# A decoder layer with a mixture of experts: the last stage by tiles in the order of the routing groups

## The chip, the cores and the metric

The kernel runs on one core of a Trainium2 chip. The metric is the device time of one execution in microseconds (us). PE is TensorE, DVE VectorE, ACT ScalarE, POOL GpSimd and SP SyncE; each executes its own instructions in order and waits for others at semaphores. SP, ACT and POOL also issue DMAs.

## The reference

One decoder layer on 512 tokens of width 1024, fp32. What matters here is the part behind the three mixers, whose sum with the input is h:

```python
t = rmsnorm(h, norm2_g)                                  # 512 x 1024
g_w, g_idx = top_k(softmax(t @ wg + bg), 1)              # one of 4 groups
e_w, e_idx = top_k(softmax((t @ we + be)[group]), 2)     # two of its 8 experts
e_w = e_w / sum(e_w) * g_w
h = h + sum over the two experts of
        (silu(t @ w_gate[e]) * (t @ w_up[e]) * e_w) @ w_down[e]     # w_*: 1024 x 256, 256 x 1024
gate = sigmoid(rmsnorm(h, ple_norm_g) @ ple_gate_w + ple_gate_b)    # 1024 x 1024
h = h + gate * (p @ ple_proj_w)                          # p: 512 x 256
return rmsnorm(h, final_norm_g)
```

## The kernel before

The first 196 us compute the projections and mixers; up to about 241 us follow the output projection, which leaves h in four SBUF tiles `h1[t]` of 128 tokens, and the routing. For each tile the inverse rms is computed, the normalised rows go to DRAM as `tnd`, and the two experts of each token are found. `Rt` keeps columns per token (weights in three bfloat16 parts, the token's number) from which a product with a one-hot matrix makes values per slot.

Then come 16 **pairs** of experts, `i` = 0 to 15. Each expert has 64 slots, so a pair fills 128 rows. For a pair, `slots_of`, `fetch` and `slot_weights` make the slots' sums (`sl`, L920), the list `idx` of tokens and their weights `wsl`; POOL gathers the rows `xg` from `tnd` by an indirect DMA (L934); `gather_T` turns them on PE (L976) and multiplies by the norm's gain. `gate_up(i)` runs over 8 blocks k of 128 of the width, two column-tiled fp32 products of 64 slots x 512 columns each (L988); `between(i)` is called between the k and puts other work into PE's order there. Silu and a product with `wsl` and the up half make `hid` (L993, L994), PE turns it (L1010), `down(i)` multiplies by the down weights (L1020), and POOL stores the rows by `idy` to `yd` in DRAM (L1033), one row for each token and each of its two experts. Pair 15's rows are not stored: the last stage adds them by a one-hot product.

The expert weights are 96 loads of 1 MiB (`slab`, L689), issued by SP in the order in which `load_units` asks for them, each into a free buffer of a ring; a buffer is given back by `free` behind the products that read it, and a load also waits for the third load ahead of it (`AHEAD`).

The ple products, p @ ple_proj_w, stand in pairs 8 to 14 by the table `PLE` (L722), with 256 columns each; their weights are asked for at pair 6. Behind pair 15 the last stage runs: `add_y` adds the rows of `yd`, `scatter` adds pair 15, `turn` turns h (L1176), the gate weights, loaded at the end of pair 14, are split into a high and a low fp32r part (`gate_hi` on ACT, L1054, `gate_lo` on DVE, L1057), and for each of the four tiles 48 fp32r products (L1197) and the chain of `finish` (L1207 to L1218) follow. The order on PE is the order of the program (`manual_schedule`); on POOL and SP a scheduler sets it.

Of the kernel before, what the change touches and what calls it, by code (L numbers as in the profile page):

```python
# [17 lines left out]
P = 128  # L18
# [11 lines left out]
PLE = {8: 5, 9: 5, 10: 5, 11: 5, 12: 4, 13: 4, 14: 4}  # L30
# [56 lines left out]
def mixers(ctx, tc, A, K, dbg):  # L87
# [363 lines left out]
    h1 = K["h1"] = [hp.tile([P, D], F32, name=f"h1_{t}") for t in range(NT)]  # L451
# [160 lines left out]
def ffn(ctx, tc, A, K, mixh, mixl, out, dbg, stage):  # L612
# [49 lines left out]
    cmf = cw.tile([P, 448], F32, name="cmf", tag="cmf")[:, :384]  # L662
# [43 lines left out]
    pl_in, eo = [], []  # L706

    def ple_load():
        pl_in.extend((big(0), unit(F32, [P, 2, D])))
        nc.sync.dma_start(pl_in[0], A["pT"])  # L710
        nc.sync.dma_start(pl_in[1], A["ple_proj_w"])

    def ple_steps():

        pT, pW = pl_in
        for j in range(8):
            t, hf = j // 2, j % 2
            p = ps("pe", "sc")
            for c in range(2):
                for k in range(2):  # L720
                    n = hf * 512 + c * 256
                    PE.matmul(p[:, c * 256:c * 256 + 256], pT[:, k * S + t * P:k * S + (t + 1) * P], pW[:, k, n:n + 256],  # L722
                              start=(k == 0), stop=(k == 1))
                    if c == k == 1:
                        SC.activation(eo[t // 2][:, t % 2, hf * 512:hf * 512 + 512], p, AF.Copy)
                    yield

    ple_left = ple_steps()

    def ple(n):  # L730
        for _ in range(n):
            next(ple_left, None)
# [21 lines left out]
    def route_in(t, hf):  # L754
# [11 lines left out]
        SC.activation(junk, h1[t][:, hs], AF.Square, accum_out=ms2[:, hf:hf + 1])  # L766

# [5 lines left out]
    def route(t):  # L773
# [664 lines left out]
```

## Time and profile before

| | us |
|---|---|
| median of 3 runs | 557.72 |
| their range | 556.37 to 564.31 |
| the profiled execution's own time | 562.7 |
| its span (first to last instruction) | 560.9 |
| PE busy in the span | 513.1 (91%) |
| DVE, ACT, POOL busy | 276.0, 209.8, 85.3 |
| begin of pair 0, end of gate-up 15 | 241.5, 475.7 |

The numbers of a profile come from one execution, here one 5 us above the median; differences are taken within it and then set against the median. A large busy share of an engine doesn't say that the engine ends last at each place: that is read from the chain of waits, stage by stage.

### The profile page before, as it was taken

The numbers are of one execution on the slowest core, as the hardware profiler recorded it, in microseconds if no ns is written. First come the engines' busy times: TensorE is split into PE (matmuls) and PEld (weight loads), VectorE is DVE, ScalarE is ACT, GpSimd is POOL, SyncE is SP. The second block draws the span as 40 slices with busy tenths as digits, with TensorE's granted clock in tenths as the row PEclk, the third lists the DMA queues.
The fourth block names the chain that finished last, engine by engine and source line by source line (L and its number), as shares of the span: only waits on it lengthen the run. The fifth ranks groups of instructions, "written<-read, shape, count | busy, mean of one in ns | idle before, by whom it ended". The sixth has DMA issues, their size and how long they took to land.

```text
span 560.9 us, 7565 instructions
## 1 busy us (share of the span) xinstructions
PE 513.1 (91%) x2713; PEld 322.1 (57%) x2713; DVE 276.0 (49%) x727; ACT 209.8 (37%) x435; POOL 85.3 (15%) x122
## 2 busy tenths in 40 slices
PE   8899999999999999979999999099999999679992
PEld 5797886877997788934333333044434333347782
DVE  6663957757846666772422222022122112687774
ACT  7466765656857444211111111001111112363442
POOL 3301121311009400002111111001111100010000
PEclk9999999999999999998999999699999999899997
DMA  8882222300449579978999999999999999861111
GB/s 305 262 330 59 74 65 78 100 1 2 134 156 420 221 294 424 356 278 327 403 417 414 393 390 377 375 409 389 395 408 420 391 415 377 348 252 37 39 38 41
DMA packets 35641, 148.82 MB, mean 265 GB/s; under 512 B 6557, under 2 KB 13597, under 8 KB 22160
## 3 DMA queue, kind: packets, MB, share of 16 engines
q1 hardware_dynamic: 29984, 137.20, 63.6%
q0 software_dynamic: 4320, 7.95, 3.8%
q10 hardware_dynamic: 1296, 3.15, 1.4%
q8 instruction: 23, 0.38, 0.3%
q14 instruction: 18, 0.15, 0.1%
HBM read 139.61 MB, written 16.25 MB: 278 GB/s over the span
## 4 chain that ended last, share of the span: by engine, by line
PE 74%; DMA 10%; DVE 7%; ACT 5%; issue 2%; POOL 1%; SPq 0%; DVEq 0%; ACTq 0%; POOLq 0%
PE gu L988 17%; PE pj L232 9%; PE dn L1020 8%; PE po L78 8%; DMA unit<-in_w_exp_dram 5%; PE pj L255 5%; PE pg L1197 4%; PE z L255 4%; PE pe L722 3%; PE z L309 2%; DMA unit<-in_ple_proj_w_dram 2%; PE po L331 2%; DVE h L1117 2%; PE x L965 1%; DMA xg<-tnd,idx 1%
## 5 line engine op out<-in xcount | busy, mean ns | idle before, releaser
L988 PE MATMUL gu<-unit,xT 128*64 128x512 f32 x512 | 116.7, 597 | 0.0
L988 PEld LDWEIGHTS gu<-unit,xT 128*64 128x64 f32 x512 | 34.5, 136 | 62.3 <-issue 60.9
L1020 PE MATMUL dn<-unit,hidT 128*64 128x512 f32 x256 | 60.1, 612 | 1.0 <-ACT hidT L1011 0.5
L232 PE MATMUL pj<-xh,wp 128*128 128x512 f32 x176 | 51.2, 398 | 0.3 <-ACT wp L67 0.3
L1197 PE MATMUL pg<-unit 128*128 128x512 f32 (+1 forms) x216 | 49.4, 384 | 1.5 <-DVE unit L1057 1.5
L993 ACT ACTIVATE sg<-gu 128x256 f32<-128x256 f32 x16 | 6.1, 384 | 106.8 <-PE gu L988 106.8
L921 DVE COPY SL<-sl 128x10 f32<-128x10 f32 (+1 forms) x17 | 2.9, 168 | 85.0 <-PE sl L920 85.0
L1197 PEld LDWEIGHTS pg<-unit 128*128 128x128 f32 x216 | 37.9, 194 | 11.2 <-DVE unit L1057 3.4
L994 DVE SCALAR_TENSOR_TENSOR hid<-sg,wsl,gu 128x256 f32<-128x256 f32 x16 | 7.7, 480 | 74.4 <-ACT sg L993 74.4
L1033 POOL DMA_INDIRECT yd<-big,idy x15 | 15.1, 1009 | 150.4 <-ACT big L1024 150.4
L232 PEld LDWEIGHTS pj<-xh,wp 128*128 128x128 f32 x176 | 32.5, 188 | 8.1 <-ACT wp L67 1.2
L1020 PEld LDWEIGHTS dn<-unit,hidT 128*64 128x64 f32 x256 | 17.3, 140 | 33.6 <-issue 28.1
L1024 ACT ACTIVATE big<-dn 128x512 f32<-128x512 f32 x30 | 17.9, 597 | 49.6 <-PE dn L1020 49.6
L68 DVE TENSOR_TENSOR wp<-wraw,wp 128x768 fp32r<-128x768 f32 (+2 forms) x28 | 25.8, 928 | 13.6 <-ACT wp L67 13.4
L722 PE MATMUL pe<-unit,big 128*128 128x256 f32 x64 | 18.4, 420 | 13.4 <-DMA unit<-in_ple_proj_w_dram 13.4
L67 ACT ACTIVATE wp<-wraw 128x768 fp32r<-128x768 f32 (+2 forms) x28 | 22.8, 817 | 20.2 <-PE pj L232 9.8
L232 PE MATMUL pj<-xl,wp 128*128 128x512 f32 x88 | 29.4, 400 | 0.0
L78 PE MATMUL po<-wo,mx 128*128 128x512 f32 x96 | 25.6, 407 | 0.0
L255 PE MATMUL pj<-wp,xh 128*128 128x384 f32 x96 | 24.8, 351 | 0.0
L78 PE MATMUL po<-unit,mx 128*128 128x512 f32 x96 | 24.1, 400 | 0.0
L977 DVE TENSOR_TENSOR xT<-xt,g2c 128x512 f32<-128x512 f32 x30 | 20.6, 688 | 6.7 <-PE xt L976 6.7
L934 POOL DMA_INDIRECT xg<-tnd,idx x15 | 15.4, 1029 | 55.7 <-issue 35.7
(293 smaller groups left out, 878.8 us busy)
## 6 DMA issues: line engine op xcount, KB each, us to landing
unit<-in_w_exp_dram SPq DMA_DIRECT2D x96, 1024.0 KB, 9.2
wraw<-in_w_in_dram SPq DMA_DIRECT2D x20, 384.0 KB, 6.1
yd<-zero SPq DMA_DIRECT2D x4, 1024.0 KB
unit<-in_ple_gate_w_dram SPq DMA_DIRECT2D x4, 1024.0 KB
unit<-yd SPq DMA_DIRECT2D x4, 1024.0 KB, 4.8
wraw<-in_w_out_dram SPq DMA_DIRECT2D x8, 256.0 KB, 2.9
h<-in_x_dram SPq DMA_DIRECT2D x4, 512.0 KB, 4.1
unit<-in_w_out_dram SPq DMA_DIRECT2D x4, 512.0 KB, 7.9
```

Of the source, the lines that this page charges most:

```text
L67: nc.scalar.activation(h, src, AF.Copy)
L68: nc.vector.tensor_tensor(l, src, h.bitcast(F32), ALU.subtract)
L78: nc.tensor.matmul(p, a[k][:, ts_], K["wo"][k][:, b, hs], start=(n == 0), stop=(n == 3 * len(ks) - 1))
L232: PE.matmul(q, a[:, i * P:(i + 1) * P], b[k], start=(n == 0), stop=(n == 3 * KC - 1))
L255: PE.matmul(p[t][:, :W_IN[j]], a[k][:, t * P:(t + 1) * P], b, start=(n == 0), stop=(n == 3 * KC - 1))
L722: PE.matmul(p[:, c * 256:c * 256 + 256], pT[:, k * S + t * P:k * S + (t + 1) * P], pW[:, k, n:n + 256], start=(k == 0), stop=(k == 1))
L934: G.indirect_dma_start(out=xg[i % 2], out_offset=None, in_=tnd, in_offset=bass.IndirectOffsetOnAxis(ap=idx[:, i:i + 1], axis=0), bounds_ch ...
L977: V.tensor_tensor(xTs[i, hf], p.rearrange("p (a b) -> p a b", a=4), g2c[:, 4 * hf:4 * hf + 4, None].to_broadcast([P, 4, P]), ALU.mult)
L988: PE.matmul(gu[64 * e:64 * e + 64], xTs[i, k // 4][:, k % 4, 64 * e:64 * e + 64], w[e][k // 4][:, 512 * (k % 4):512 * (k % 4) + 512], star ...
L1020: PE.matmul(dn[64 * e:64 * e + 64], hT[:, f, 64 * e:64 * e + 64], w[e][2][:, 1024 * f + 512 * hf:1024 * f + 512 * hf + 512], start=(f == 0 ...
L1024: SC.activation(o[:, 512 * hf:512 * hf + 512], dn, AF.Copy)
L1197: PE.matmul(p, hT[t][:, a, ks], gw[k][:, b, hs], start=start and n == 0, stop=stop and n == len(ab) - 1)
```

## The change

Five things change together.

- **Inverse rms at the slots.** `hd` takes the place of `tnd`: the rows of h as they are, stored by ACT without waiting for the inverse rms. The inverse rms goes into three more columns of `Rt` and comes out per slot as `rsl`; `wsl` is multiplied by its square. `gate_up` ends with two ACT and two DVE instructions instead of one each.
- **Tokens ranked by group.** `ranks()` in pair 1 gives each token a rank in the order of the four groups, and stores the list through DRAM (`perm_d`) into `perm`: four indirect stores and one load, all on POOL. Rows of p, of h (`load_h`) and of yd (`load_y`) are gathered by `perm` on POOL. Tiles of the last stage are tiles of this order, so tile 0 needs no pair behind 7 and tile 1 none behind 11.
- **Where the work stands.** The table `WORK` has three numbers for a pair: steps ahead of gate-up, between its k, and behind it. A step is a group of four transposes or one product of 512 columns. ple stands in pairs 4 to 8, tile 0 of the last stage in 9 to 12, tile 1 in 13 to 15; tiles 2 and 3 follow pair 15.
- **Gate weights unsplit.** 16 fp32 products of 512 columns for a tile instead of 48 fp32r ones; the gate weights are loaded behind pair 5, in the stream of the expert loads.
- The output is stored by rows with an indirect DMA on POOL. The two buffers that held `h1` join the ring of the weights, and the longer-lived tiles (p, ple weights, gate weights, rows, h, y) take buffers of it.

```diff
-PLE = {8: 5, 9: 5, 10: 5, 11: 5, 12: 4, 13: 4, 14: 4}
+WORK = {4: (0, 3, 1), 5: (0, 3, 1), 6: (0, 3, 1), 7: (0, 3, 1), 8: (0, 1, 1),
+        9: (1, 3, 1), 10: (1, 3, 1), 11: (1, 3, 1), 12: (0, 2, 1), 13: (1, 4, 1), 14: (1, 4, 1), 15: (1, 4, 1)}
...
-        SC.activation(sg, gu[:, :256], AF.Silu)
-        V.scalar_tensor_tensor(hid, sg, wsl[:, i:i + 1], gu[:, 256:], ALU.mult, ALU.mult)
+        SC.activation(hid, gu[:, :256], AF.Copy, scale=wsl[:, i:i + 1])
+        SC.activation(sg, gu[:, :256], AF.Sigmoid, scale=rsl[:, i:i + 1])
+        V.tensor_tensor(hid, hid, gu[:, 256:], ALU.mult)
+        V.tensor_tensor(hid, hid, sg, ALU.mult)
...
+    ring.extend(((K["hp"], "h0"), (K["hp"], "h1")))
     load_units()
...
+    def ranks():
...
+        for t in range(NT):
+            G.indirect_dma_start(out=perm_d, out_offset=bass.IndirectOffsetOnAxis(ap=rki[:, t:t + 1], axis=0), in_=tok[:, t:t + 1],
+                                 in_offset=None, bounds_check=S - 1, oob_is_err=False)
+        G.dma_start(perm, perm_d.rearrange("(t p) o -> p (t o)", p=P))
...
+    def ple_load():
+        pl["p"], pl["w"] = unit(F32, [P, 2, D]), unit(F32, [P, 2, D])
+        nc.sync.dma_start(pl["w"], A["ple_proj_w"])
+        for t in range(NT):
+            rows_of(pl["p"][:, 0, t * 256:t * 256 + 256], A["p"], perm[:, t:t + 1], S)
...
+    def load_y(t):
+        if t not in ys:
+            ys[t] = unit(F32, [P, 2, D])
+        for r, ix in enumerate((perm, perm2)):
+            rows_of(ys[t][:, r], yd, ix[:, t:t + 1], 2 * S)
...
+            for k in range(KC):
+                PE.matmul(p, q["x"][:, 0, k * P:k * P + P], gr[k // 2][:, k % 2, hs], start=(k == 0), stop=(k == KC - 1))
...
+            if i == 1 and k == 6:
+                ranks()
+            if k in (1, 3, 5, 6)[:n]:
+                run(work, 1)
+            if i in (8, 12) and k == 6:
+                load_y(i // 4 - 2)
...
-        ple(PLE.get(i, 1) - 1)
+        ahead, _, behind = WORK.get(i, (0, 0, 0))
+        run(work, ahead)
         gate_up(i, between(i))
         free(*(slab[6 * i + n] for n in (0, 3, 1, 4)))
         if i == 15:
             break
-        if i == 6:
+        if i == 2:
             ple_load()
+        if i == 5:
+            for j in range(4):
+                gate_load(j)
         if i == 7:
-            eo += [unit(F32, [P, 2, D]) for _ in range(2)]
+            rows_load()
+            load_h(0)
...
         load_units()
         gather_T(i + 1, 1)
-        if i in PLE:
-            ple(1)
+        run(work, behind)
         down(i, lambda n: gather_T(i + 1, 0))
```

PE's order in pair 4, before, from the slots' sums to the down products (`gu` gate-up, `xt` a turn of xg, `ht` the turn of hid, `dn` down):

```order
L920 MATMUL sl<-pr,Dm 128x10
L988 MATMUL gu<-unit,xT 64x512 x14
L976 MATMUL xt<-ident,xg 128x128 x4
L1010 MATMUL ht<-ident,hid 128x128 x2
L976 MATMUL xt<-ident,xg 128x128 x4
L1020 MATMUL dn<-unit,hidT 64x512 x8
```

The same place in the changed kernel (L1120 turns p, L1110 is a ple product):

```order
L911 MATMUL sl<-pr,Dm 128x13
L982 MATMUL gu<-unit,xT 64x512 x2
L1120 MATMUL xt<-ident,unit 128x128 x4
L982 MATMUL gu<-unit,xT 64x512 x4
L1120 MATMUL xt<-ident,unit 128x128 x4
L982 MATMUL gu<-unit,xT 64x512 x4
L1110 MATMUL pe<-unit 128x512
L982 MATMUL gu<-unit,xT 64x512 x4
L970 MATMUL xt<-ident,xg 128x128 x4
L1110 MATMUL pe<-unit 128x512
L999 MATMUL ht<-ident,hid 128x128 x2
```

Three steps have moved between the products of gate-up, two of them turns that read the gathered p, and one between the turn of xg and that of hid.

POOL's order from pair 3 to pair 5, before (the numbered names in brackets are the DMA rings and engines that an instruction waits for):

```order
L934 DMA xg<-tnd,idx 128x1024 [waits DMASW1_49,DVE_49,PE_49]
L1033 DMA yd<-big,idy 1024x1024 [waits DMASW4_49,Activation_49]
L934 DMA xg<-tnd,idx 128x1024 [waits DMASW3_49,DVE_49,PE_49]
L1033 DMA yd<-big,idy 1024x1024 [waits DMASW6_49,Activation_49]
L934 DMA xg<-tnd,idx 128x1024 [waits DMASW5_49,DVE_49,PE_49]
```

The same stretch in the changed kernel:

```order
L925 DMA xg<-hd,idx 128x1024 [waits DMASW3_49,DVE_49,PE_49]
L1084 DMA perm<-tok,rki 512x1 [waits DMASW0_49]
L1022 DMA yd<-big,idy 1024x1024 [waits DMASW1_49,Activation_49]
L925 DMA xg<-hd,idx 128x1024 [waits DMASW6_49,DVE_49,PE_49]
L1086 DMA perm_2559<-perm 128x4x1 [waits DMASW3_49]
L1090 DMA unit<-in_p_dram,perm_2559 128x256 [waits DMASW6_49]
L1090 DMA unit<-in_p_dram,perm_2559 128x256 x2
L1090 DMA unit<-in_p_dram,perm_2559 128x256 [waits DMASW2_49]
L1022 DMA yd<-big,idy 1024x1024 [waits DMASW4_49,Activation_49]
```

The load of perm and the four gathers of p now stand behind the gather xg(6), which is issued in pair 4, and ahead of the store yd(4).

PE's order at the change from pair 8 to pair 9 in the changed kernel (L1173 turns h of tile 0, L1198 is a gate product); before, nothing stands there but gate-up, sums, turns, down and ple:

```order
L1009 MATMUL dn<-unit,hidT 64x512 x8
L1173 MATMUL xt<-ident,unit 128x128 x4
L982 MATMUL gu<-unit,xT 64x512 x2
L911 LDWEIGHTS Dm
L911 MATMUL sl<-pr,Dm 128x13
```

The first turn of tile 0 stands between the down products of pair 8 and gate-up of pair 9.

## Rows read from the trace of the kernel before

**Rows 1.** Windows: stretch, length, busy us (x instructions) of PE PEld DVE ACT POOL, PEclk, DMA, GB/s

```profile
350.00:365.00 15.00, 1.64 (x7) 0.98 (x4) 0.00 (x0) 0.60 (x1) 1.01 (x1) 0.61 0.99 378
365.00:476.00 111.00, 110.02 (x529) 44.10 (x527) 22.57 (x88) 18.89 (x38) 13.13 (x13) 0.99 1.00 403
476.00:561.00 85.00, 62.50 (x283) 46.15 (x283) 58.21 (x93) 34.73 (x68) 5.28 (x8) 0.92 0.32 125
```

**Rows 2.** Chain of waits in order of time: start us, us, what (x records)

```profile
144.60 0.86 PE z L354 x2
...
299.08 0.86 PE gu L988 x4
299.94 0.19 PE sl L920 x4
300.13 6.21 PE gu L988 x28
308.29 3.65 PE dn L1020 x16
...
352.46 11.28 DMA unit<-in_ple_proj_w_dram
363.88 3.54 PE pe L722 x8
...
380.42 1.93 PE pe L722 x8
...
395.36 1.92 PE pe L722 x8
...
473.85 1.89 PE gu L988 x8
```

**Rows 3.** Waits of the SP queue: us in total, times, longest

```profile
SPq L689 <- DMA unit<-in_w_exp_dram: 219.4, 84, 9.3
```

**Rows 4.** Waits of PE from 241 to 476 us

```profile
PE pe L722 <- DMA unit<-in_ple_proj_w_dram: 13.4, 1, 13.4
...
PE xt L976 <- DMA xg<-tnd,idx: 1.9, 1, 1.9
```

**Rows 5.** Timeline at the end of gate-up of pair 5

```profile
319.08 0.66 PE L976 MATMUL xt<-ident,xg 128*128 128x128 f32 x4
319.28 0.38 ACT L993 ACTIVATE sg<-gu 128x256 f32<-128x256 f32 x1 [6.67 <-PE gu L988]
...
319.70 0.48 DVE L994 SCALAR_TENSOR_TENSOR hid<-sg,wsl,gu 128x256 f32<-128x256 f32 x1 [5.00 <-ACT sg L993]
...
320.24 0.44 PE L1010 MATMUL ht<-ident,hid 128*128 128x128 f32 x2 [0.50 <-DVE hid L994]
```

**Rows 6.** Timeline of POOL in pair 4

```profile
300.03 1.00 POOL L1033 DMA_INDIRECT yd<-big,idy  x1 [10.12 <-ACT big L1024]
301.75 1.01 POOL L934 DMA_INDIRECT xg<-tnd,idx  x1 [0.72 <-issue]
```

**Rows 7.** Issue to landing: gathers (L934), stores (L1033), and a page row

```profile
DMA to landing us min/median/max: 4.9/8.8/11.2
...
DMA to landing us min/median/max: 7.7/8.6/9.3
...
out_dram<-unit ACTq DMA_DIRECT2D x4, 256.0 KB, 2.9
```

**Rows 8.** Timeline of the last products' chain in the last stage

```profile
549.43 0.43 DVE L1209 TENSOR_TENSOR unit<-unit 128x256 f32<-128x256 f32 x1 [0.48 <-ACT unit L1208]
...
551.65 0.48 DVE L1207 SCALAR_TENSOR_TENSOR unit<-pg,rsp,rows 128x256 f32<-128x256 f32 x1
...
554.88 0.72 ACT L1215 ACTIVATE unit<-unit,rsl 128x512 f32<-128x512 f32 x1 [0.85 <-POOL rsl L61]
...
555.64 0.34 ACTq L1216 DMA_DIRECT2D out_dram<-unit  x1
```

**Rows 9.** Groups of the last stage: out<-in xcount, busy, mean ns, idle before

```profile
L1117 DVE TENSOR_TENSOR h<-h,unit 128x1024 f32<-128x1024 f32 x8 | 9.8, 1223 | 5.3 <-DMA unit<-yd 5.1
```

More of the change, by code (lines that the diff above doesn't have):

```diff
@@ L703, in ffn @@
     load_units(2)
[L706 to L732, printed above, removed]
     V.tensor_copy(cm.rearrange("p a b -> p (a b)"), cmf)
     V.tensor_tensor(rw, rw, g2c[:, :, None].to_broadcast([P, KC, 36]), ALU.mult)
-    tnd = dram.tile([S, D], F32, name="tnd")
-    Ab = mw.tile([P, NT, 32], BF, name="Ab")
-    pr_ = cw.tile([P, 448], F32, name="pr", tag="cmf")
+    hd = dram.tile([S, D], F32, name="hd")
+    Ab = mw.tile([P, NT, 40], BF, name="Ab")
+    pre = mw.tile([P, NT, 4], F32, name="pre")
+    pr_ = cw.tile([P, 576], F32, name="pr", tag="cmf")
     posA = pr_[:, :128].rearrange("p (t e) -> p t e", t=NT)
@@ new lines, in ple_steps @@
+    def ple_steps(pT, n):
+        for j in range(8):
+            t, hf = j // 2, j % 2
+            p = ps("pe", "sc")
+            for c in range(0, 512, n):
+                for k in range(2):
+                    m = hf * 512 + c
+                    PE.matmul(p[:, c:c + n], pT(t, k), pl["w"][:, k, m:m + n], start=(k == 0), stop=(k == 1))
+                    if c + n == 512 and k:
+                        SC.activation(eo[t // 2][:, t % 2, hf * 512:hf * 512 + 512], p, AF.Copy)
+                    yield
@@ new lines, in begin, with add_y, mean_sq @@
+    def begin(t):
+        T[t] = dict(h=hs_[t], x=unit(F32, [P, 2, D], slot_of[id(ys[t])][0]), e=eo[t // 2][:, t % 2], n=t)
+    def add_y(t, rs=(0, 1)):
+        for r in rs:
+            V.tensor_tensor(hs_[t], hs_[t], ys[t][:, r], ALU.add)
+    def mean_sq(ms, m):
+        if ms is None:
+            ms = small("msq", 1)
+            V.tensor_scalar(ms, m, 1.0 / D, EPS, ALU.mult, ALU.add)
+        else:
+            V.scalar_tensor_tensor(ms, m, 1.0 / D, ms, ALU.mult, ALU.add)
+        return ms
@@ new lines, in by_group, with tile_work, all_work @@
+    def by_group(q, ot):
+        G.indirect_dma_start(out=out, out_offset=bass.IndirectOffsetOnAxis(ap=perm[:, q["n"]:q["n"] + 1], axis=0), in_=ot, in_offset=None,
+                             bounds_check=S - 1, oob_is_err=False)
+    def tile_work(t):
+        add_y(t)
+        begin(t)
+        for hf in range(2):
+            turn(T[t], hf)
+            yield
+        rms(T[t])
+        yield from finish(T[t], by_group, ((0, 512), (512, 512)), "sc")
+    def all_work():
+        yield from ple_work()
+        free(pl["p"], pl["w"])
+        for t in range(2):
+            yield from tile_work(t)
@@ L1096, in between, with count_beyond @@
+    def count_beyond():
+        on = ov["on"] = mw.tile([1, 1], I32, name="on")
+        po = ps("pov", "xt")
+        PE.matmul(po[:1, :1], ov["om"], ones[:, :1], start=True, stop=True)
+        V.tensor_copy(on, po[:1, :1])
     def between(i):
+        n = WORK.get(i, (0, 0, 0))[1]
         def go(k):
@@ L1263, in ffn, with behind_down @@
-    ov_slots = ring[:4]
-    junk, h3s = (unit(F32, shape, slot) for shape, slot in zip(([P, 2, 512], [P, 4, 512]), ring[4:]))
-    SC.preload_act_table_set("sigmoid_and_others")
-    rms(0)
-    tail(sums)
+    run(work, WORK[15][2])
+    def behind_down(n):
+        if n < 2:
+            add_y(2, (n,))
+            run(work, 1)
+    down(15, behind_down)
+    for t in (2, 3):
+        if t == 3:
+            add_y(3)
+        begin(t)
+        for hf in range(2):
+            scatter(t, hf)
+        if t == 2:
+            prep(T[2])
+            count_beyond()
```

386 lines of the change are left out of this document (214 added, 172 removed).

## The prediction, made before the changed kernel had run

> **What bounds the kernel now.** I read the windows first [rows 1]. In the second half of the expert pairs, from 365 to 476 us, PE is busy for 110.02 of 111.00 us, while the DMA share is 1.00. So PE and the weight stream are both full there, and the next view has to say which ends last. Ahead of it lies a stretch of 15 us in which PE does 1.64 us of work; in the last stage (476 to 561) PE has 62.50 of 85.00 us, DVE 58.21, and the DMA share is 0.32.
>
> The chain of waits [rows 2] gives the pair as a unit: pair 4 begins at 299.08 and ends with its down products, 3.65 us from 308.29 on, at 311.94. That is 12.86 us a pair, all PE: gate-up, the turn of hid, down. In pair 8 the chain leaves PE for the load of the ple weights, which lands at 363.74; PE waits 13.4 us [rows 4] and then needs 3.54 us for eight ple products that take 1.93 us in pair 9, with a mean granted clock of 0.61 in that stretch, part of it at the lower of the two levels (1.2 and 2.4 GHz) behind an idle PE [rows 1, 2]. From there a pair lasts 14.94 us (380.42 to 395.36). The wait list of the SP queue [rows 3] shows that the weight loads wait 219.4 us for earlier loads and little for anything else; the DMA is a second bound, just under the first. The end of gate-up in pair 15 is at 475.7 [rows 2]; the 85.2 us from there to 560.9 are the tail.
>
> **The change, part by part.** I sum in two pieces, up to the end of gate-up 15 and the tail.
>
> *Pairs, PE alone.* Without ple and its wait, pair 15 would begin at 299.08 + 11 x 12.86 = 440.5 and its gate-up, 0.86 + 0.19 + 6.21 us and a last small step [rows 2], would end at 447.9. The program before has 28 us above that: 17.0 in pair 8, the rest ple at 2 us a pair.
> An unsplit fp32 product of 512 columns on the full array is in this program already: two records at 144.60, 0.86 us [rows 2]. Put between column-tiled products it also costs a change of the array's use and back; four ten-column products with both changes cost 0.19 us at 299.94 [rows 2]. So 1.05 us for each inserted step; for a group of four transposes, 0.66 us [rows 5], I take 0.6. The step behind gate-up costs nothing: it stands where PE waits for hid (0.50 us idle there [rows 5]) and that wait grows, by the next point. hid had one ACT and one DVE instruction after gate-up (0.38 and 0.48 us), and now has two ACT and two DVE ones; the added DVE product of 128x256 at 0.43 [rows 8] and its hand-over make 0.48 us a pair, on the path.
> By WORK that gives: pair 0 -0.9 (below), 1 to 3 1.4, 4 2.7, 5 to 7 3 x 3.63 = 10.9, 8 1.5, 9 3.8, 10 and 11 2 x 4.68 = 9.4, 12 2.6, 13 4.8, 14 5.7, 15 5.25; together 47.2. Gate-up 15 ends at 495.1 if nothing waits. The -0.9: in pair 0 the first gather waits for the normalised rows; these are now stored unscaled, some 3 us earlier, and PE's wait for xg was 1.9 us in all [rows 4].
>
> *Added wait 1, rows of p.* The transposes of p stand in PE's order at the second k of pair 4, ahead of the rest of its gate-up. In pair 4 PE comes to them at 299.6 + 1.9 = 301.5. On POOL the load of perm stands behind xg(6), which before is issued at 301.75 [rows 6] and now at about 302.3, since its index comes from the same pair. perm is issued at 303.3 in the same queue. xg lands 4.9, 8.8 or 11.2 us after its issue (minimum, median, maximum) [rows 7]; at the median perm is there at about 312, then POOL issues the gathers of p one by one at 1.0 us each [rows 6], and the second, which the first group needs, goes out at 313.0. With 5.5 us, nearer to the minimum because these rows are a quarter of xg's, it lands at 318.5: a stall of **17.0 us** on PE. With 4.9 us for both steps it is 12.6, with 8.8 for p too 20.3, and below nothing it can't go, as perm can't be issued before xg(6). A stall of that kind also cost 3.54 - 1.93 = 1.6 us of clock. Behind POOL's wait are queued yd(4) and xg(7), which PE needs only two pairs later, so they cost nothing.
> The Trainium skill, "DMA: Bandwidth & Descriptors", section "Anatomy of one DMA — SWDGE (gpsimd) path", gives about 2.0 us plus the bytes at 436 GB/s for such a DMA; by that estimate xg(6) and perm land near 305.5, p at 308.7, and the stall is 7 us. The trace disagrees for this kernel: the same kind of gather took at least 4.9 us here [rows 7].
>
> *Added waits 2 and 3, rows of yd.* Tile 0 needs yd of pair 7, tile 1 that of pair 11. yd(i) is issued about 1 us after the start of the next pair (300.03 in pair 4 [rows 6]) and lands 8.6 us later [rows 7]: 9.7 us into pair 8. Only then POOL issues the two gathers; the second goes at 10.7 and lands at about 19.2, and DVE adds it in 1.22 us [rows 9]. PE wants the turned tile behind down(8), at 12.86 + 1.5 = 14.4. That is a stall of **6 us** (2.4 with landings of 4.9, 8.7 with 11.2). In pair 13 the same sum against 12.86 + 2.6 = 15.5 gives **5 us** (1.3 to 7.6). Queued behind these on POOL are yd(8) and xg(11), with a pair's slack.
>
> *Weights.* Gate weights, rows, h and y rows add 9.5 MiB ahead of the last expert load. At 403 GB/s [rows 1] that is 24.7 us on a last arrival at about 475, less 5 for the two more slots of the ring: 494.5, or 505 where the ring is full during the stall. PE with its waits comes to 495.1 + 17.0 + 1.6 + 6 + 5 = **524.7**, so the stream doesn't decide.
>
> *Tail.* hid, turn and down start 2.4 us after gate-up 15 (1.9 before, by the steps of [rows 5], plus 0.48), down takes 3.65 [rows 2], the scatter and its additions end at 9.0, the turns of tile 2 at 10.6. Then 32 products of 0.86 us and 1.3 us of transposes: 39.4. From the last product to the scaling 3.2 us (551.65 to 554.88 [rows 8]), scaling 0.6, the store by rows from POOL 6.4 us (between 4.9 and 8.8, nearer the low end since little else moves), and about 2 us from the last landing to the end as before (555.64 + 0.34 + 2.9 to 560.9 [rows 7, 8]). Together **51.5** instead of 85.2. Gone are the split of the gate weights on ACT and DVE, the wait of 5.1 us for yd [rows 9], and two of four tiles with 48 products each.
>
> Sum: 524.7 + 51.5 = 576.2 against a span of 560.9, +15.3. The profiled execution (562.7) is 5 us above the median of 557.7; I add the difference to the median: **573 us**, 2.7% slower.
>
> **The rivals.**
> A. *Short landings.* DMA work gets thinner while PE stalls, and each landing comes at the minimum of the rows, 4.9 us. Then the stalls are 12.6, 2.4 and 1.3, gate-up 15 ends at 495.1 + 12.6 + 1.6 + 3.7 = 513.0, the tail at 50.0, span 563, median about 560: no change that a measurement of this kernel can tell (about 2%). For it: the rows of p are small. Against it: the median of 15 gathers in the pairs is 8.8, beside a weight stream like this one. The skill's figure quoted above would go further, to about 551.
> B. *The other side: PE never waits.* If perm is there in pair 3, for instance because the queue issues it while xg(6) still waits for its index, p is in place at 302; and if yd lands by the middle of a pair, the turns are on time. Then only the weight stream (494.5 to 505) and PE (495.1) count, and the span is 495.1 to 505 + 51.5 = 546.6 to 556.5, median 543 to 553, about 546. It decides from a p landing below 302 on. Against it stands POOL's order, in which one engine issues all of these.
> C. *Longer.* DVE and ACT have the chains of the moved tiles to do between the hid of two pairs, on engines that execute in order; 1 us more in each of pairs 9 to 15 (a DVE instruction of 128x1024 is 1.22 us [rows 9]) and stalls at their upper ends (20.3, 8.7, 7.6) give +7 + 8.6: 588.
> That the change doesn't do what it says has no room here: the two tiles do stand in the pairs in PE's order.
>
> **How the numbers follow.** The forecast has 0.50, A 0.22, B 0.13, C 0.15. The forecast's own range is 566 to 580. The range leaves out most of B and the upper half of C: 553 to 584. More than 2% slower begins at 568.9: C and most of the forecast, 0.56; faster than 546.6 is half of B, 0.06; the rest, 0.38, is within 2%.
>
> **What would show it.** In the profile after, a wait of PE for rows of p of 10 to 20 us near 302, with a low clock behind it; waits of PE for the turned tile of about 6 us at the start of pair 9 and 5 at that of pair 13; inserted products at 0.86 us; end of gate-up 15 near 525, and 51 us behind it. I am wrong if p comes early (B), if the landings are short (A), or if weights are what PE waits for in pairs 9 to 15.

## The result and the profile after

The changed kernel took 631.15 us (627.34 to 631.93, four runs) against 558.75 for the kernel before; the ratio, by the means of all runs (six of the changed kernel), is 1.1262, 95% interval 1.118 to 1.1343. Run again later, beside the experiments, it took 626.62 us, ratio 1.1132 (1.1076 to 1.1189). It is 11 to 13% slower, where 2.7% was forecast and 584 us was the upper end of the range. The span of its profiled execution is 625.6 us; gate-up 15 ends at 556.5 instead of 475.7, and the tail behind it takes 69.1 us instead of 85.2.

Windows of the changed kernel, columns as in [rows 1]: pair 4, pair 5, pairs 8 and 9, pairs 12 and 13, and three stretches of the tail:

```profile
307.18:345.39 38.21, 18.09 (x76) 6.07 (x74) 4.29 (x18) 4.52 (x9) 6.89 (x7) 0.73 0.76 263
345.39:362.99 17.60, 16.80 (x72) 5.39 (x70) 4.11 (x17) 3.61 (x7) 2.07 (x2) 1.00 0.94 366
398.19:422.51 24.32, 15.58 (x72) 5.55 (x69) 6.66 (x20) 4.74 (x10) 5.53 (x5) 0.91 0.95 381
422.51:442.01 19.50, 18.70 (x76) 5.93 (x75) 5.47 (x20) 2.62 (x7) 1.68 (x3) 0.93 0.95 384
479.00:503.49 24.49, 16.77 (x74) 5.74 (x70) 9.73 (x26) 5.98 (x13) 7.05 (x7) 0.93 0.97 385
503.49:524.67 21.18, 20.38 (x77) 6.14 (x76) 3.92 (x9) 2.63 (x7) 3.67 (x5) 0.92 0.71 274
556.50:564.20 7.70, 1.42 (x4) 0.38 (x4) 4.56 (x9) 3.08 (x7) 0.56 (x1) 0.84 0.03 9
564.20:570.10 5.90, 5.87 (x17) 1.68 (x18) 2.29 (x3) 0.62 (x2) 1.24 (x1) 0.63 0.22 89
570.10:605.50 35.40, 30.36 (x74) 14.51 (x75) 15.49 (x28) 6.53 (x16) 2.91 (x4) 0.86 0.00 0
```

A pair that took 12.86 us now takes 17.60 with three steps between its products; pair 4 takes 38.2, with PE busy in half of it. In these three stretches of the tail PE has a granted clock of 0.63 to 0.86. The wait list of PE says where it stood, to be read beside [rows 4]:

```profile
PE xt L1120 <- DMA unit<-in_p_dram,perm: 19.3, 2, 18.7
PE ht L999 <- DVE hid L990: 16.1, 15, 2.9
PE xt L1173 <- DVE unit L1158: 14.3, 2, 7.9
PE dn L1009 <- ACT hidT L1000: 5.4, 1, 5.4
PE xt L1173 <- DVE unit L1174: 3.9, 2, 3.1
PE xt L970 <- DMA xg<-hd,idx: 3.5, 1, 3.5
```

The first is the wait for the rows of p in pair 4, the third the two for the rows of yd ahead of pairs 9 and 13 (7.9 and 6.4). The last is the wait for the first gather in pair 0, which was 1.9 us before [rows 4]. No line of it names the expert weights. POOL's timeline up to the gathers of p, where [rows 6] had a store and a gather for each pair:

```profile
294.30 0.99 POOL L1084 DMA_INDIRECT perm<-tok,rki  x1 [11.55 <-DMA perm<-tok,rki]
...
303.12 1.01 POOL L1084 DMA_INDIRECT perm<-tok,rki  x1 [5.20 <-DMA perm<-tok,rki]
...
310.05 1.04 POOL L925 DMA_INDIRECT xg<-hd,idx  x1 [0.70 <-issue]
312.26 0.82 POOL L1086 DMA_DIRECT2D perm<-perm  x1 [1.17 <-DMA perm<-tok,rki]
325.18 1.04 POOL L1090 DMA_INDIRECT unit<-in_p_dram,perm  x1 [12.10 <-DMA perm<-perm]
```

Each store of ranks waits for the landing of the one before; the load of perm waits for the last of them and then lands 12.7 us after its issue, though it is 2 KB; only then the gathers of p go out. Two rows of the DMA issues give the landings of p and perm, and the view of line L925 those of the gathers xg:

```profile
unit<-in_p_dram,perm POOLq DMA_INDIRECT x4, 2.8
perm<-perm POOLq DMA_DIRECT2D x1, 2.0 KB, 12.7
...
DMA to landing us min/median/max: 4.4/9.2/14.1
```

The longest of these gathers, 14.1 us, is xg(6), issued at 310.05, 2.2 us ahead of the load of perm in the same queue. It lands at 324.15, and perm 0.8 us behind it; in the five other traces that show both landings perm is 0.6 to 0.8 us behind xg(6) too, issued 1.5 to 3.1 us after it. The load had waited only 1.17 us for the last store of ranks. So of the chain it is mainly the place of the load behind xg(6) that makes the wait, as the traces read, and not the four stores; no run has the one without the other.

The end of gate-up in pair 5, to be set beside [rows 5]:

```profile
354.93 1.46 PE L982 MATMUL gu<-unit,xT 128*64 128x512 f32 x6
...
356.46 0.47 ACT L987 ACTIVATE hid<-gu,wsl 128x256 f32<-128x256 f32 x1 [4.23 <-PE gu L982]
356.84 0.47 ACT L988 ACTIVATE sg<-gu,rslot 128x256 f32<-128x256 f32 x1
357.02 0.69 DVE L971 TENSOR_TENSOR xT<-xt,g2c 128x512 f32<-128x512 f32 x1 [8.32 <-PE xt L970]
357.62 0.41 DVE L989 TENSOR_TENSOR hid<-hid,gu 128x256 f32<-128x256 f32 x1
358.07 0.42 DVE L990 TENSOR_TENSOR hid<-hid,sg 128x256 f32<-128x256 f32 x1
358.55 0.44 PE L999 MATMUL ht<-ident,hid 128*128 128x128 f32 x2 [0.71 <-DVE hid L990]
...
359.51 1.51 PE L1009 MATMUL dn<-unit,hidT 128*64 128x512 f32 x6
```

The kernel before at the same place, beside [rows 5] (where hid is at 319.70):

```profile
318.55 0.60 PE L988 MATMUL gu<-unit,xT 128*64 128x512 f32 x2
...
320.10 0.68 DVE L977 TENSOR_TENSOR xT<-xt,g2c 128x512 f32<-128x512 f32 x1
...
321.15 3.65 PE L1020 MATMUL dn<-unit,hidT 128*64 128x512 f32 x16
```

DVE multiplies the turned xg (L971) ahead of hid; before, hid came first. From the last product of gate-up to down it is 3.12 us (356.39 to 359.51), before 2.00 (319.15 to 321.15). It is 3.12 in pairs 2 and 3 too, where no step stands behind gate-up, so that step costs nothing here, as predicted. The start of the tail, with the chain of tile 1's second half on DVE, ACT and POOL:

```profile
558.20 0.74 DVE L1202 SCALAR_TENSOR_TENSOR unit<-pg,rsp,unit 128x512 f32<-128x512 f32 x1
558.43 0.41 PE L999 MATMUL ht<-ident,hid 128*128 128x128 f32 x2 [0.92 <-DVE hid L990]
558.98 0.63 ACT L1203 ACTIVATE unit<-unit 128x512 f32<-128x512 f32 x1 [1.61 <-DVE unit L1202]
...
561.09 0.63 ACT L1206 ACTIVATE unit<-unit 128x512 f32<-128x512 f32 x1 [1.48 <-DVE unit L1205]
...
563.29 0.61 ACT L1212 ACTIVATE unit<-unit,rsl 128x384 f32<-128x384 f32 x1 [1.48 <-POOL rsl L64]
...
563.82 0.36 ACT L1000 ACTIVATE hidT<-ht 128x256 f32<-128x256 f32 x1
564.23 5.77 PE L1009 MATMUL dn<-unit,hidT 128*64 128x512 f32 x16 [5.39 <-ACT hidT L1000]
```

The copy of the turned hid (L1000) stands behind ACT's part of that chain (L1203, L1206, L1212); PE waits 5.4 us, and the 16 records of down then take 5.77 us instead of the 3.65 of [rows 2].

### The profile page after: what moved, and what is told of

Read it like the earlier page. It is cut to its first block, busy times and chain, and to the rows that moved or that the text cites. A ratio compares the mean times of both kernels' runs of the same rounds, so it can differ in the third digit from the quotient of the medians.

```text
span 625.6 us, 7465 instructions
## 1 busy us (share of the span) xinstructions
PE 543.0 (87%) x2609; PEld 302.3 (48%) x2609; DVE 276.2 (44%) x797; ACT 199.9 (32%) x435; POOL 111.9 (18%) x147
## 3 DMA queue, kind: packets, MB, share of 16 engines
q0 software_dynamic: 6976, 16.87, 7.5%
## 5 line engine op out<-in xcount | busy, mean ns | idle before, releaser
L982 PE MATMUL gu<-unit,xT 128*64 128x512 f32 x512 | 128.6, 621 | 0.0
L1009 PE MATMUL dn<-unit,hidT 128*64 128x512 f32 x256 | 64.2, 647 | 6.5 <-ACT hidT L1000 5.4
L971 DVE TENSOR_TENSOR xT<-xt,g2c 128x512 f32<-128x512 f32 x30 | 20.7, 691 | 109.3 <-PE xt L970 109.3
L1198 PE MATMUL pg<-unit 128*128 128x512 f32 (+1 forms) x144 | 66.8, 591 | 0.0
L982 PEld LDWEIGHTS gu<-unit,xT 128*64 128x64 f32 x512 | 32.2, 139 | 69.8 <-issue 68.3
L987 ACT ACTIVATE hid<-gu,wsl 128x256 f32<-128x256 f32 x16 | 7.6, 474 | 120.2 <-PE gu L982 107.1
L1198 PEld LDWEIGHTS pg<-unit 128*128 128x128 f32 x144 | 26.2, 200 | 35.3 <-issue 34.3
L71 DVE TENSOR_TENSOR wp<-wraw,wp 128x768 fp32r<-128x768 f32 (+2 forms) x28 | 25.8, 928 | 13.8 <-ACT wp L70 13.5
L912 DVE COPY SL<-sl 128x13 f32<-128x13 f32 (+2 forms) x17 | 2.9, 171 | 51.8 <-PE sl L911 51.8
L970 PE MATMUL xt<-ident,xg 128*128 128x128 f32 x120 | 20.2, 294 | 3.5 <-DMA xg<-hd,idx 3.5
L1173 PE MATMUL xt<-ident,unit 128*128 128x128 f32 x32 | 6.5, 338 | 18.3 <-DVE unit L1158 14.3
L970 PEld LDWEIGHTS xt<-ident,xg 128*128 128x128 f32 x120 | 14.4, 149 | 14.9 <-issue 14.9
```

The source lines that it names most:

```text
L71: nc.vector.tensor_tensor(l, src, h.bitcast(F32), ALU.subtract)
L970: PE.transpose(p[:, k * P:(k + 1) * P], xg[i % 2][:, (4 * hf + k) * P:(4 * hf + k + 1) * P], ident)
L971: V.tensor_tensor(xTs[i, hf], p.rearrange("p (a b) -> p a b", a=4), g2c[:, 4 * hf:4 * hf + 4, None].to_broadcast([P, 4, P]), ALU.mult)
L982: PE.matmul(gu[64 * e:64 * e + 64], xTs[i, k // 4][:, k % 4, 64 * e:64 * e + 64], w[e][k // 4][:, 512 * (k % 4):512 * (k % 4) + 512], star ...
L1009: PE.matmul(dn[64 * e:64 * e + 64], hT[:, f, 64 * e:64 * e + 64], w[e][2][:, 1024 * f + 512 * hf:1024 * f + 512 * hf + 512], start=(f == 0 ...
L1198: PE.matmul(p, q["x"][:, 0, k * P:k * P + P], gr[k // 2][:, k % 2, hs], start=(k == 0), stop=(k == KC - 1))
```

## The experiments

Ratios are to the kernel before, run on the same chip (561 to 561.5 us). Against the second measurement of the changed kernel, 1.1132, differences under 0.6% are not told apart by the time; there the trace decides. Traces differ by chance too: pair 0 begins between 240.8 and 245.4 us, though hardly an edit touches what stands ahead of it, and gate-up 15 of the same kernel ended at 556.5 and at 558.4. The second measurement is of the unedited kernel:

> The changed kernel again, unedited, so that the other edits are set against a run beside them. Theory: its ratio to before is the first one, 1.118 to 1.134. Rival 'the first measurement lay high': the spans of the profiles (625.6 here, 623.4 and 623.5 with edits that took 2 us off the trace) say that it is nearer 1.115.

Measured 1.1132 (1.1076 to 1.1189), span 627.4: the rival is right, the first measurement lay high by about 1%. In this run the waits were 17.5, 9.9 and 7.6.

**ple one pair later.**

```diff
-WORK = {4: (0, 3, 1), 5: (0, 3, 1), 6: (0, 3, 1), 7: (0, 3, 1), 8: (0, 1, 1),
+WORK = {5: (0, 4, 1), 6: (0, 4, 1), 7: (0, 4, 1), 8: (0, 2, 1),
```

> The changed kernel with the ple work in pairs 5 to 8 instead of 4 to 8 (same steps, one pair later; only the table is edited). Theory 'PE in line' (each wait in PE's order and the low clock behind it come off the end one for one): the wait for the rows of p, 18.7 us in pair 4, falls to at most 4 us, pair 4 loses some 5 us of slow products as well, end of gate-up 15 at 532 to 536 instead of 556.5, time some 20 to 24 us shorter, near 609. Rival 'weights': the stream of weights has used that wait to get ahead; PE waits for expert weights in pairs 8 to 13 instead and the time falls by less than 10 us.

Measured 1.0992 (1.0931 to 1.1052), span 619.7, gate-up 15 at 551.6. The time fell by some 7 us (626.62 to 619.73): the rival's number, less than 10, but not for its reason, since PE's wait list names no expert weights. The wait only fell to 12.2 us, since the scheduler had also moved POOL. Its timeline in this kernel:

```profile
312.25 0.82 POOL L1086 DMA_DIRECT2D perm<-perm  x1 [1.44 <-DMA perm<-tok,rki]
321.99 1.03 POOL L1022 DMA_INDIRECT yd<-big,idy  x1 [8.92 <-ACT big L1013]
323.74 1.04 POOL L925 DMA_INDIRECT xg<-hd,idx  x1 [0.72 <-issue]
325.08 1.01 POOL L1090 DMA_INDIRECT unit<-in_p_dram,perm  x1 [0.30 <-issue]
```

The gathers of p went out at the same time as before the edit, now behind a store and a gather of the next pair, and landed 9.8 to 10.1 us later instead of 2.8. Two things differ there, and no run tells them apart: the gather xg of 512 KB stands 1.3 us ahead in the same queue (it took 10.1 us, and the first p landed 1.3 us behind it), and the DMA share is 1.00 instead of 0.28.

**Silu in pairs 0 to 7.**

```diff
-        SC.activation(hid, gu[:, :256], AF.Copy, scale=wsl[:, i:i + 1])
-        SC.activation(sg, gu[:, :256], AF.Sigmoid, scale=rsl[:, i:i + 1])
-        V.tensor_tensor(hid, hid, gu[:, 256:], ALU.mult)
-        V.tensor_tensor(hid, hid, sg, ALU.mult)
+        if i < 8:
+            SC.activation(sg, gu[:, :256], AF.Silu, scale=rsl[:, i:i + 1])
+            V.scalar_tensor_tensor(hid, sg, wsl[:, i:i + 1], gu[:, 256:], ALU.mult, ALU.mult)
+        else:
...
```

In these pairs `wsl` is the weight times the inverse rms, not its square; the other pairs keep the four lines.

> The changed kernel with the old form of hid in pairs 0 to 7: one Silu on ACT with the inverse rms as its scale, one DVE instruction with the weight times the inverse rms. Theory 'two more instructions are the 1.1 us between gate-up and down (3.1 instead of 2.0)': 3.1 goes back to 2.0 to 2.1 in eight pairs, 8 to 9 us shorter, near 622, less where the step behind gate-up (pairs 4 to 7) no longer fits under the wait: at worst 4 us shorter. Rival 'the order on DVE' (the turned xg is multiplied before hid): it stays at 2.7 or more, and the gain is under 3 us.

Measured 1.1087 (1.1029 to 1.1145), span 620.9. From gate-up to down it is 2.67 us in pairs 2 to 7, not 2.0: the two instructions are 0.45 of the 1.12 us. That is the rival's stretch; gate-up 15 ends 3.7 us earlier, between the rival's 3 and the 4 of the theory at worst. In pair 8, the first with the new form, ACT loads a table between Copy and Sigmoid (ACT_TABLE_LOAD, 1.28 us), and the stretch is 4.26.

**DVE's order at hid.**

```diff
+        with ExitStack() as behind:
+            if i > 0:
+                behind.enter_context(tc.issue_after(K["hid", i - 1].ins))
             V.tensor_tensor(xTs[i, hf], p.rearrange("p (a b) -> p a b", a=4),
...
```

> The changed kernel with DVE's order as it was before at the end of gate-up: the turned xg is multiplied behind the last product of hid, not ahead of the first. Theory 'order on DVE is 0.6 of the 1.1 us that a pair has lost between gate-up and down': 3.1 falls to about 2.5 in 15 pairs, 8 to 10 us shorter. Rival 'the two added instructions are all of it': it stays at 3.0 or more and the time doesn't move by more than 2 us.

Measured 1.1087 (1.1036 to 1.1139), span 623.4. The stretch falls to 2.84 us, 0.28 less: between the two theories, since the first product on DVE now waits for the sigmoid. With both edits (g4b_all below) it is 2.09 us in pairs 2 and 3, so the order is worth 0.6 there once the two instructions are gone; in pairs 4 to 7 it is 2.41, since the step behind gate-up no longer fits into the wait. The wait at pair 9 grew from 7.9 to 9.1 meanwhile.

**Last step of tile 1.**

```diff
-... 15: (1, 4, 1)}
+... 15: (1, 4, 0)}
```

> The changed kernel with the last step of tile 1 (its 16th product and the chain of DVE and ACT behind it) emitted behind the copy of the turned hid of pair 15 instead of ahead of it. Theory 'ACT's order': the 5.4 us for which down(15) waits go, and with them the low clock of down(15) (5.8 instead of 3.65): 6 to 8 us shorter, near 624. Rival 'the chain only moves': ACT's chain now delays the copies of down's results, and the tail gets at most 3 us shorter.

Measured 1.1177 (1.1115 to 1.124), span 623.5: no difference in the time. Gate-up 15 ends at 556.55, down starts 3.2 us later instead of 7.8 and takes 3.65, but the tail is only 2.2 us shorter: the rival. PE's wait list has this line instead:

```profile
PE sc L1255 <- ACT big L1017: 2.7, 1, 2.7
```

**Tile 0 in pairs 10 to 12.**

```diff
-        9: (1, 3, 1), 10: (1, 3, 1), 11: (1, 3, 1), 12: (0, 2, 1), 13: ...
+        10: (1, 4, 1), 11: (1, 4, 1), 12: (1, 4, 1), 13: ...
```

> The changed kernel with tile 0 of the last stage in pairs 10 to 12 (six steps each) instead of 9 to 12. Theory 'PE in line': the wait of 7.9 us ahead of pair 9 for the rows of yd goes, and with it some 1.5 us of low clock: 8 to 10 us shorter, near 622. Rival 'the wait moves': tile 0 now ends where tile 1 begins, the wait ahead of pair 13 grows or DVE delays hid in pairs 10 to 12, and at most 4 us are left.

Measured 1.0907 (1.0835 to 1.0978), span 609.6, 16 us less: more than the 8 to 10 expected. Only one wait for yd is left, ahead of pair 13, and it is smaller (2.9 us). Gate-up 15 ends 12.7 us earlier: 7.9 and 3.5 of the two waits, the rest low clock behind the first. The tail is 3.3 us shorter, for which the runs show no cause.

**p without the list.**

```diff
-            rows_of(pl["p"][:, 0, t * 256:t * 256 + 256], A["p"], perm[:, t:t + 1], S)
+            nc.sync.dma_start(pl["p"][:, 0, t * 256:t * 256 + 256], A["p"][t * P:(t + 1) * P, :])
```

> The changed kernel with the rows of p loaded by SP in the order of the tokens, as plain loads, instead of gathered by the list of ranks; the ple term is then added to the wrong tokens, so this part of the computation is changed. Theory 'the chain on POOL (four scatters, one load, four gathers, each waiting for the one before) is the wait of pair 4': the 18.7 us go, with 4 to 5 us of low clock; 20 to 24 us shorter. Rival 'the wait is only moved': the stream of weights, which was 0.76 busy during the wait, or the rows of yd at pairs 9 and 13 take most of it, gain under 10 us.

Measured 1.0857 (1.0803 to 1.0912), span 611.8. Pair 4 takes 16.66 us instead of 38.2: the wait of 18.7 and 2.9 us of low clock. But the waits for yd grow to 13.6 and 6.8, and pair 4 began 2.0 us later in this run, so that gate-up 15 ends 13.3 us earlier, not 21:

```profile
PE xt L1173 <- DVE unit L1158: 20.4, 2, 13.6
```

**The list made on PE.** The one-hot of each token's rank, built by DVE, is multiplied with the tokens' numbers (16 products, pair 2), in place of four stores and a load:

```diff
-            G.indirect_dma_start(out=perm_d, out_offset=bass.IndirectOffsetOnAxis(ap=rki[:, t:t + 1], axis=0), in_=tok[:, t:t + 1], ...)
-        G.dma_start(perm, perm_d.rearrange("(t p) o -> p (t o)", p=P))
+            V.tensor_tensor(ohx[0][:, t], iota64[:, None, :].to_broadcast([P, 8, 64]), ra[:, :, None].to_broadcast([P, 8, 64]), ALU.is_equal)
...
+                PE.matmul(pq[:, 2 * j:2 * j + 2], ohx[0][:, t, 2 * j:2 * j + 2].rearrange("p b s -> p (b s)"), Rt[:, t, 0, 6:8], ...)
```

> The changed kernel with the list of ranks turned round on PE (16 products of a one-hot matrix with the tokens' numbers in pair 2) instead of by four indirect stores and a load on POOL; p is gathered as before. Theory 'the chain of DMAs on POOL is the wait of pair 4': p is there before pair 4, the 18.7 us go with 3 us of low clock, end of gate-up 15 about 16 to 20 us earlier (some of it given back at pair 9, where without the chain the wait grew from 7.9 to 13.6 us with plain loads of p). Rival 'gathers of p are late by themselves': a wait of 8 us or more stays in pair 4.

Measured 1.0766 (1.0709 to 1.0823). In this kernel the entries lay beyond the tables (an offset of 1024 was missing), so no row was gathered or stored by the list (the POOL queue moved 7.96 MB instead of 16.87); its time leaves that traffic out. With the offset:

> The changed kernel with the list of ranks made on PE, now with the right entries. Theory 'the chain of DMAs on POOL is the wait of pair 4': no wait for p above 2 us in pair 4, gate-up 15 ends 14 to 20 us earlier (536 to 543), the wait at pair 9 is larger than the 7.9 us of the changed kernel. Rival 'gathers of p are late by themselves': a wait of 8 us or more stays in pair 4.

Measured 1.0871 (1.0817 to 1.0925), span 605.7, gate-up 15 at 538.3, 18.2 us earlier; p is there in pair 4, and the wait at pair 9 is 11.1:

```profile
PE xt L1186 <- DVE unit L1171: 17.5, 2, 11.1
```

So the chain of DMAs was the wait of pair 4, and the first theory holds. The edit takes out the stores and the load together; which of them held the gathers up is read from the traces alone.

**Tile 3 turned early.**

```diff
-    run(steps, 10)
+    run(steps, 5)
     prep(T[3])
```

> The changed kernel with the turns of tile 3 five products into tile 2 instead of ten, so that DVE's part of a turn stands ahead of the chain behind the first half and not behind it. Theory 'order on DVE in the tail': PE's wait of 3.1 us for the turned tile 3 goes, and some low clock with it: 3 to 5 us shorter. Rival 'rows of yd': the sum with yd for tile 3 isn't there any earlier, no change.

Measured 1.1087 (1.1044 to 1.1131), span 617.6. Up to gate-up 15 the program is that of the changed kernel (gate-up 15 ended 2.5 us earlier, by chance); the tail takes 63.7 us instead of 69.1, 69.0 in the second trace, and the wait falls to 0.8:

```profile
PE xt L1173 <- DVE unit L1174: 1.6, 2, 0.8
```

**Gate weights unsplit, alone, in the kernel before.**

```diff
-        for n, (a, b) in enumerate(ab):
-            PE.matmul(p, hT[t][:, a, ks], gw[k][:, b, hs], ...)
+        PE.matmul(p, hT[t][:, 0, ks], gr[k // 2][:, k % 2, hs], start=start, stop=stop)
```

> The kernel before with one part of the change alone: gate weights unsplit, 16 fp32 products of 512 columns for a tile instead of 48 fp32r ones, the gain of the norm multiplied into the turned h. On PE 64 products of 0.86 us (55 us) stand against 192 of 0.233 us (45 us), so 10 us more; gone is the split, behind which the first product had to wait (499.9 at the earliest complete set). Theory 'price and split cancel': within 3 us of before. Rival 'PE ends last': 8 to 11 us slower. Rival 'the split was the wait': 4 us faster or more.

Measured 1.0001 (0.9972 to 1.0029): the first theory. The windows, the second from the first gate product to the last one's end, show one bound taking the other's place; PE starts at 483.1, 11.4 us behind gate-up 15, and is then full:

```profile
471.70:483.10 11.40, 6.87 (x30) 2.77 (x30) 6.13 (x9) 4.58 (x9) 0.00 (x0) 1.00 0.87 349
483.10:544.50 61.40, 61.11 (x181) 31.96 (x181) 39.87 (x71) 16.57 (x39) 3.81 (x7) 1.00 0.26 98
```

**Both tiles out of the pairs.**

```diff
-8: (0, 1, 1), 9: (1, 3, 1), 10: (1, 3, 1), 11: (1, 3, 1), 12: (0, 2, 1), 13: (1, 4, 1), 14: (1, 4, 1), 15: (1, 4, 1)}
+8: (0, 1, 1), 15: (0, 0, 0)}
```

> The changed kernel with both tiles taken out of pairs 9 to 15: their 36 steps run behind pair 15 with the other two tiles. Theory 'PE is the bound in the pairs, and a step put there costs more (1.2 us and the waits around it) than in the tail (0.9 to 1.0)': pairs 9 to 15 get 43 us of steps and 14 us of waits shorter, gate-up 15 ends near 498, the tail grows from 69 to about 103 us, in all 20 to 26 us shorter. Rival 'the pairs had room': weights then hold PE up in pairs 9 to 15, gate-up 15 ends at 515 or later, and the time is within 5 us of the changed kernel's or longer.

Measured 1.1249 (1.1193 to 1.1304), span 631.9: the rival. Gate-up 15 ends at 515.5, not 498, since weights now hold PE up (granted clock 0.97 in pairs 12 to 15), and the tail takes 116.5:

```profile
PE xt L1172 <- DVE unit L1157: 16.5, 2, 8.3
PE gu L981 <- DMA unit<-in_w_exp_dram: 5.8, 4, 2.7
```

The first line is a wait in the tail, for the sums with yd of two tiles, that neither theory had. It is more than the 13.5 us by which the tail exceeds the expected 103, so the time doesn't show what a step costs in the pairs and in the tail.

**All repairs together.** The list on PE, tile 0 in pairs 10 to 12, tile 1 with (0, 4, 1) at pair 13 and its last step behind the copy of the turned hid, Silu in pairs 0 to 7, DVE's order, tile 3 early. First with the list whose entries lie beyond the tables:

> All repairs together: ranks on PE, tile 0 in pairs 10 to 12, tile 1 from k = 1 of pair 13, its last step behind the copy of the turned hid, Silu in pairs 0 to 7, DVE's order at hid as before, tile 3 turned early. Theory 'the waits are one part, the steps in the pairs the other': waits of PE in the pairs fall below 8 us in all, gate-up 15 ends at 512 to 520, tail 62 to 66 us, time 577 to 588, still 3 to 5% slower than before. Rival 'the waits are all of it': 565 or less, within 1% of before. Rival 'weights': gate-up 15 can't end ahead of 515, where it ended with both tiles taken out, and PE waits for expert weights for 10 us or more.

Measured 1.0293 (1.0248 to 1.0338), without the traffic of the list. With the right list:

> All repairs together, with the right list: ranks on PE, tile 0 in pairs 10 to 12, tile 1 from k = 1 of pair 13, its last step behind the copy of the turned hid, Silu in pairs 0 to 7, DVE's order at hid as before, tile 3 turned early. Theory 'waits are one part, steps in the pairs the other': waits of PE for DMAs in the pairs below 8 us in all, gate-up 15 ends at 511 to 520, time 577 to 590, 3 to 5% above before. Rival 'the waits are all of it': 565 or less.

Measured 1.0325 (1.0272 to 1.0378), 579.2 us, span 577.3, gate-up 15 at 516.3, tail 61.0: the first theory's numbers. PE's longest waits for DVE and for a DMA, and the windows of pairs 4 to 7, 10 to 12, 13 to 15 and of the tail:

```profile
PE ht L1009 <- DVE hid L1000: 11.1, 8, 3.0
...
PE xt L973 <- DMA xg<-hd,idx: 2.2, 1, 2.2
```

```profile
302.00:368.60 66.60, 65.38 (x287) 21.95 (x284) 14.80 (x64) 13.14 (x25) 10.05 (x10) 1.00 1.00 397
401.80:461.00 59.20, 56.08 (x225) 17.40 (x226) 18.84 (x63) 9.61 (x21) 8.56 (x9) 1.00 1.00 405
461.00:516.30 55.30, 50.72 (x191) 15.18 (x187) 15.03 (x40) 8.50 (x19) 11.92 (x13) 0.97 0.69 268
516.30:577.30 61.00, 41.93 (x128) 21.91 (x127) 29.35 (x54) 14.08 (x34) 6.84 (x8) 0.85 0.08 32
```

No wait for p or yd over 1 us is left, and PE and the DMAs are both full in pairs 4 to 7 and 10 to 12, but not in 13 to 15 (50.72 of 55.30 us, DMA share 0.69). PE still waits 11.1 us for hid in pairs 8 to 15: in pair 8 behind the table load named above, in pair 14 (3.0 us) behind tile 1's chain on ACT and DVE.

**The same with both tiles in the tail.**

> The repaired kernel with both tiles in the tail instead of the pairs. Theory 'once the waits are gone the weight stream leaves room in the pairs': gate-up 15 can't end ahead of 500 to 510, because the weights hold PE up, the tail grows by 34 to 45 us, so 20 to 35 us longer than the repaired kernel. Rival 'a step costs as much in the pairs as in the tail, as the unrepaired kernel showed': within 6 us of it.

Measured 1.0753 (1.0687 to 1.0818), span 601.2, 24 us more than with the tiles in the pairs: the first theory's time, but neither of its parts. Gate-up 15 ends at 493.1, ahead of its 500 to 510 (though PE waits 7.7 us for weights), and the tail takes 108.1, 47 us more and not 34 to 45. As in the unrepaired kernel, 15.4 us of that tail are waits for the sums with yd (8.2 and 7.2). No version that beat the kernel before was found.

## Why the prediction was wrong

The direction, the places of the three waits and their mechanism were right. What failed is the sum: the price of the hand-over behind gate-up, that of an inserted step, and the tail, which had no room for chains on ACT and DVE that hold PE up. Of 49.4 us between the forecast span (576.2) and the measured one, 31.8 lie ahead of the end of gate-up 15 (524.7 against 556.5) and 17.6 in the tail (51.5 against 69.1).

- **Wait 1, rows of p**: 17.0 forecast, 18.7 measured, clock 1.6 forecast, 2.9 (pair 4 against f2_p_direct). The mechanism, a load of perm that lands behind xg(6), was right, and g3b_perm_pe shows that the wait goes with the chain. That the number came close is luck in part: perm took 12.7 us, 3.9 more than the 8.8 of the sum, and p 2.8, 2.7 less than its 5.5. The four stores of ranks, which the sum leaves out, cost at most 1.2.
- **Waits 2 and 3, rows of yd**: 6 and 5 forecast, 7.9 and 6.4 measured. Right in place. The store of yd took 7.8 us instead of 8.6, but the second gather 11.4 at pair 9 and 11.5 at pair 13 instead of 8.5, and PE came later.
- **Weights**: "the stream doesn't decide" was right: PE never waited for them in the changed kernel. With the tiles taken out it did (f3_tiles_tail, g5_all_tiles_tail).
- **"Make 0.48 us a pair"**: failed. The two added instructions cost 0.45 (e2_hid_silu), but DVE's order also changed at that place, by the scheduler, and together they are 1.12: 0.64 more in 15 pairs, 9.6 us. I read PE's and POOL's order, not DVE's.
- **"So 1.05 us for each inserted step"**: failed by 0.16. In pair 5 gate-up with three steps takes 11.0 us against 7.37 without: 3.63 / 3 = 1.21. With some 42 steps that is up to 6.7 us. The price of the product (0.86) is right where it stands in a row (f4_before_unsplit); that of the change came from a row of four ten-column products.
- **"Pair 0 -0.9"**: failed. The first gather did not wait for the rows but for the index: it was issued at 244.29 instead of 244.60, landed after 9.2 us instead of 7.5, and PE's wait for it is 3.5 us instead of 1.9.
- **Low clock and the first pairs**: about 10 us of the 31.8 are left (31.8 - 9.6 - 6.7 - 5.0 for the three waits). By the lengths of the pairs, as an estimate, 5.5 of them are in pairs 0 to 3: 1.3 in pair 0, 2.5 in pair 1, where hid comes 2.9 us late behind the work of the ranks on DVE, and 1.7 in pair 3, where down takes 5.35 us instead of 3.65. Low clock is 1.3 at pair 4 (2.9 instead of 1.6) and, behind the waits for yd, some 1.2 and 1.7 in gate-up 9 and 13, against the same steps elsewhere (1.21 us for a product, 0.74 for a turn by pair 4 of f2_p_direct). About 1 is in pairs 10 and 12, where DVE has tile 0's chain between the two halves of hid and the stretch to down is 3.65 us.
- **Tail "51.5"**: failed, and it had no upper bound. ACT's order cost 5.4 us and the low clock of down 2.1 more at its place, of which 2.2 in all were to be had by moving one step (e3_last_step); DVE's order at tile 3 cost 5.4, its wait of 3.1 and low clock behind it (g2_t3_early). The scatter of tile 3, 1.8 us, is not in the sum; the rest is in products of 1.0 us instead of 0.86 at a clock of 0.86 between the waits. The last product ends 55.9 us into the tail and not at 39.4; what follows it was right within 1.1 us.

One reading was wrong without harm: the eight records of a ple row [rows 2] are four products of 256 columns, not eight.

My rival C had the right cause, chains on DVE and ACT that delay PE, and gave it 1 us in seven pairs. It was applied to the pairs with tiles alone, and neither to the tail nor to pairs 0 to 8. By the Trainium skill, "DMA: Bandwidth & Descriptors", section "Anatomy of one DMA — SWDGE (gpsimd) path", such a DMA takes about 2.0 us plus the bytes at 436 GB/s, an estimate of 2.3 us for 128 KB. The trace comes near it, with 2.8 us, for the gathers of p, while no other gather was under way and the DMA share was 0.28; the same gathers took 9.8 to 10.1 us in e1_ple_late, behind a gather of 512 KB and with a share of 1.00.

Where the change could have paid is not settled by the last two kernels. With the waits for DMAs repaired, tiles in the pairs are worth 24 us against tiles in the tail, but 15.4 of these are the waits for yd in that tail, and no run has it without them. Against the kernel before, the repaired one still ends gate-up 15 40.6 us later (516.3 against 475.7) and has a tail 24.2 us shorter: 16.4 us slower. The kernel before had 28 us between its PE work without ple and the end of gate-up 15, half of it used by ple already [rows 2, 4]; the 42 steps ahead of gate-up or inside it, 50 us at 1.2, don't go in there. What stays open is why the clock fell at pair 3 in the first trace and not in the second (down 5.35 and 3.65 us).

## What to carry to other kernels

Before moving work from a tail into a loop, count the idle time that its engine has there, less what the move adds to each iteration and to the transfers; here PE had too little of it. Compare the order on every engine, DVE and ACT too, since a scheduler that is given one more instruction may put an old one ahead of the chain that all wait for. A chain of small dependent DMAs is priced by the landings of the big ones ahead of it in its queue, and a stage summed term by term needs an upper bound as much as any wait.

## What the runs showed of the hardware

- A 2 KB load from POOL took 12.7 us to land, 0.8 us behind a gather of 512 KB that was issued 2.2 us ahead of it in the same queue, with the DMA share at 0.69 to 0.80. Indirect stores of 128 words each took 8.6 to 12.3 us, among gathers and stores of 512 KB and with a share of 0.96 to 1.01. Gathers of 128 KB took 2.8 us with no larger one under way and a share of 0.28.
- A Silu of 128x256 with a per-row scale read from SBUF took 0.47 us (e2_hid_silu); without one, 0.38 [rows 5]. Between Copy and the first Sigmoid behind it ACT loaded a table for 1.28 us (pair 8 of e2_hid_silu).
- An unsplit fp32 product of 128x128x512 took 0.86 us in a row of its kind and 1.21 between column-tiled ones, against three products 0.233 us apart for its split form in the kernel before; in the whole kernel before, split and unsplit made no difference (1.0001, 0.9972 to 1.0029).
